# GpSimd's scaling of the attention weights with a second operation, K's late half not at step 4 for the fifth pair, and the last pair of a group coupling one step later

## The chip, the cores and the metric

The kernel runs on one core of one Trainium2 chip. The metric is the device time of one execution in microseconds (us), and the time before is the median of three runs. The core's engines work side by side, each through its own list of instructions in order: TensorE (PE in the profile, its weight loads PEld), VectorE (DVE), ScalarE (ACT), GpSimd (POOL) and SyncE (SP), which starts DMAs. ScalarE starts some DMAs too.

## The reference

One layer of a hybrid decoder, 512 tokens by 1024 channels, all in float32. Cut to what matters here:

```python
h = rms_norm(x, norm_mix_pre)
z_rwkv, z_nsa, z_gate = split(h @ w_in)
# RWKV-7, 16 heads of 64
z = z + (prev - z) * mu                        # prev: the token before
r, k, v, ... = split(z)
state = state * w_t + (state @ a_t) b_t + v_t k_t ;  y_t = state @ r_t
# sparse attention, 16 heads of 64: compressed, selected, window
p_c = masked_softmax(s_c);  p_s = masked_softmax(s_s);  p_w = masked_softmax(s_w)
o_b = gb[0] * (p_c @ v_cmp) + gb[1] * (p_s @ vg) + gb[2] * (p_w @ vwb)
m = sigmoid(g_a) * (o_a @ w_branch_rwkv) + sigmoid(g_b) * (o_b @ w_branch_nsa)
x = x + rms_norm(m @ w_out, norm_mix_post)
u_gate, u_val = split(causal_dwconv(rms_norm(x) @ ffn_up))
x = x + rms_norm((silu(u_gate) * u_val) @ ffn_down)
```

With 512 tokens there are 8 blocks of 64 and all of them are selected, and the window of 512 reaches every earlier token, so the selected and the window branch are both full causal attention, each with keys and values of its own.

## The kernel before, in words

**Precision.** A float32 product is made of three matmuls on split operands: high weight by high input, high weight by low input, low weight by high input (lines 306, 307, 308, for each of 8 slices k of the contraction). The weights come by DMA as float32 in halves of 512 columns and are split by `split_to`: ScalarE copies the high part (L124), GpSimd subtracts to get the low part (L162). Three buffers of each kind go round.

**Stages.** After the norm come the small projections, then, in one long stage, the projections of RWKV's r, k and v for eight pairs of heads (a pair is 128 columns), with the RWKV scan in chunks of 64 tokens in two groups of four pairs (GP = 4) running beside them and beside the projections of the gates (`gsteps`, tiles gt0.. and gt1..), of attention's keys (`khl`, tiles kst) and of its queries. Then come attention, eight pairs of heads one after the other (`score`, `values`), the merge with w_out, and the gated FFN.

**What orders the work.** The Python code is made of generators. One list of them, the fill, holds projections, whose step is one k, so three matmuls. Other generators (`prep`, `couple`, `invert`, `recur`, `finish`) run as threads beside the fill: for each step of the fill a thread advances by its rate (0.6 for couple). A `yield` more in a thread thus puts what follows some projection matmuls later. From the resulting sequence a scheduler makes each engine's list; an instruction given to `keep_in_program_order` stays where the code has put it, others may be moved a little. PSUM is handed out in tiles of one bank: the projections (k, r, v, gt, kst) share a small pool, and a new tile takes the bank that was released first.

**What the change touches.**
- `inputs(p)` (from L493) projects k, r and v of pair p. Token shift is done at the eviction in two halves: `shift_a` on ScalarE writes K = (1 - mu) k (L333), `shift_b` on VectorE adds mu times the token before, from the same PSUM bank (L336). For K, `shift_b` is issued at step SK = 4 of r's projection and kept there. R and V have both halves right at their eviction.
- `couple` (L581) makes of a pair's tiles what the scan needs: it multiplies AR's second half on GpSimd, yields twice, then transposes V (tiles pv, L140), multiplies KB by AR on TensorE (tiles g, L605), masks the products on VectorE (L608) and sends two kinds of blocks by DMA (ld and l2, L617 and L618). AR's first half was made on VectorE in `prep` (L570). After it come more transposes (pt), the tile LV and the tile bv with its DMA bvd.
- `invert` inverts the triangular blocks of a group: four loads of XL (L650), which read the ld blocks back, a copy into PSUM on ScalarE (XP, L655), and a chain of multiplications and additions on VectorE (L660, L662) that is covered by projections.
- `gsteps` projects a gate and evicts it on ScalarE (L478) with a store behind it on ScalarE's queue (gtd, L479).
- `score` (L1051) handles two heads of attention. Per query block of 128 it makes the scores, subtracts the maximum and takes the exponential of both branches (tiles p, 512, 384, 256 or 128 columns); `norm` (L1063) then scales each p in place by one number per row, its gate divided by its sum, which lies in a small tile stt: the selected branch on VectorE, the window branch on GpSimd, both at L1073. `values` transposes p (tiles pt, L140) and multiplies by the values (o, L1146). The compressed branch (sc, L1037 to L1049) runs beside it on VectorE and GpSimd, and its transposes are the tile pct.

Of the kernel before, what the change touches and what calls it, by code (L numbers as in the profile page):

```python
# [13 lines left out]
OP = mybir.AluOpType  # L14
# [18 lines left out]
GP = 4  # L33
PR, CR, IY, FR = 0.6, 0.5, 31, 0.5
ID, IE, RD, RR, NG0, NQ1, PX, FN = (30, 30), (54, 54), (67, 67), (1.05, 0.85), 8, 4, 3, 1.15
NW, NU, PA, SK = 13, 3, 0.25, 4
# [6 lines left out]
def hybrid_layer(ctx: ExitStack, tc: tile.TileContext, a, out, dbg=None, stop=None):  # L43
# [288 lines left out]
    def shift_a(p, o, mc, n=128):  # L332
        sc.activation(o, p[:n], AF.Copy, scale=omm[:n, mc:mc + 1])  # L333
# [159 lines left out]
    def inputs(p, o):  # L493
        K = o.K = rw.tile([128, S], F32, tag="K", name=f"K{p}", bufs=2)
        pk = pj(f"k{p}")
        yield from proj_steps(4 + 3 * p, f"k{p}", pk)
        shift_a(pk, K, 8 + p)
        R = o.R = rw.tile([128, S], F32, tag="R", name=f"R{p}", bufs=1)
        pr = pj(f"r{p}")
        for i, _ in enumerate(proj_steps(3 + 3 * p, f"r{p}", pr)):  # L500
            if i == SK:
                tc.keep_in_program_order(shift_b(pk, K, 8 + p))
            yield
        shift(pr, R, p)
        VW = o.VW = rw.tile([128, 64 + S], F32, tag="V", name=f"V{p}", bufs=1)
        po.memset(VW[:, 0:64], 0.0)
        pv = pj(f"v{p}")
        yield from proj_steps(5 + 3 * p, f"v{p}", pv)
        shift(pv, VW[:, 64:], 16 + p)
        o.lh = rw.tile([128, 256], F32R, tag="lh", name=f"lh{p}", bufs=1)  # L510
        o.ll = rw.tile([128, 256], F32R, tag="ll", name=f"ll{p}", bufs=1)
        split_to(a["lwa"][p], o.lh, o.ll, f"lw{p}", 256)
# [68 lines left out]
    def couple(p, o, gr, i):  # L581
        R, VW, Q, EC, KB = o.R, o.VW, o.Q, o.EC, o.KB
        AR = gr.AR[i]

        if Q is not None:
            sc.activation(AR[:, 0, :], Q, AF.Copy)
        po.tensor_tensor(AR[:, 1, :].rearrange(c8, t=64), R.rearrange(c8, t=64), EC[:, :, 1:65], op=OP.mult)
        sc.activation(gr.Dc[:, i], EC[:, :, 64], AF.Copy)
        yield
        yield  # L590
        for q in range(2):
            pv = px(f"pv{p}{q}")
            for j in range(4):
                c = 4 * q + j
                tr(pv[:, j * 128:(j + 1) * 128], VW[:, c * 64:c * 64 + 128], ident)
            pvv = pv.rearrange("p (c h f) -> p c h f", h=2, f=64)
            sc.activation(gr.UV[64:128, 4 * q:4 * q + 4, i], pvv[64:128], AF.Copy)
        m4 = mask.rearrange("p (s t) -> p s t", t=64)[:, None].to_broadcast([128, 4, 2, 64])
        for q in range(2):
            gh = [(pz, py)[q](f"g{p}{q}{h}") for h in range(2)]  # L600
            for j in range(4):
                c = 4 * q + j
                for h in range(2):
                    hs = slice(h * 64, (h + 1) * 64)
                    te.matmul(gh[h][:, j * 128:(j + 1) * 128], KB[hs, c].rearrange("p s t -> p (s t)"),  # L605
                              AR[hs, :, c * 64:(c + 1) * 64], start=True, stop=True)
            for h in range(2):
                ve.tensor_tensor(gr.GS[:, 0:2 + i:1 + i, 4 * q:4 * q + 4, h].rearrange("p s c t -> p c s t"),  # L608
                                 gh[h].rearrange("p (c s t) -> p c s t", s=2, t=64), m4, op=OP.mult)
            po.tensor_tensor(KB[:, 4 * q:4 * q + 4].rearrange("p c s t -> p c (s t)"),  # L610
                             KB[:, 4 * q:4 * q + 4].rearrange("p c s t -> p c (s t)"),
                             EC[:, 4 * q:4 * q + 4, 64:65].to_broadcast([128, 4, 128]), op=OP.mult)
        yield
        yield
        for b in range(2):
            bs = slice(b * 32, (b + 1) * 32)
            sy.dma_start(gr.ld[b, i].rearrange("c h i t -> i (c h) t"), gr.GS[bs, 0, :, :, bs])  # L617
        sy.dma_start(gr.l2[i].rearrange("c h i t -> i (c h) t"), gr.GS[0:32, 0, :, :, 32:64])  # L618
        yield
        yield  # L620
        pt = [px(f"pt{p}{q}") for q in range(2)]
        for q in range(2):
            for j in range(4):
                c = 4 * q + j
                m = tr(pt[q][:, j * 128:(j + 1) * 128], KB[:, c].rearrange("p s t -> p (s t)"), ident)
                if c == 0:
                    tc.keep_in_program_order(m)
            sc.activation(gr.BKT[i][:, 4 * q:4 * q + 4, :], pt[q].rearrange("p (c f) -> p c f", f=128), AF.Copy)
        pl = py(f"pl{p}")
        for c in range(8):  # L630
            for h in range(2):
                te.matmul(pl[h * 64:(h + 1) * 64, c * 64:(c + 1) * 64], gr.GS[64:128, 0, c, h, :],
                          gr.UV[64:128, c, i, h, :], start=True, stop=True)
        sc.activation(gr.LV[:, i], pl.rearrange(c8, t=64), AF.Copy)
        pbo = py(f"pbo{p}")
        te.matmul(pbo, onesr, o.rbh, start=True, stop=False)
        te.matmul(pbo, onesr, o.rbl, start=False, stop=True)
        bv = rw.tile([128, S], F32, tag="T", name=f"bv{p}", bufs=NT)
        ve.tensor_tensor(bv, pbo, VW[:, 64:], op=OP.mult)
        sy.dma_start(bvd[p], bv)  # L640
        yield
        yield
# [268 lines left out]
    for g in range(2):  # L911
        group_tiles(g)
        for i in range(GP):
            p = GP * g + i
# [136 lines left out]
    def score(p8, o):  # L1051
        kt = kst[p8 // 2]
        cmp_ = compressed(p8, o)
        next(cmp_)
        rh, st = [], []
        for e in range(2):
            h = 2 * p8 + e
            rh.append(nw.tile([128, S], F32, tag="rh", name=f"rh{h}", bufs=4))
            po.tensor_scalar(rh[e], dist, float(2.0 ** (-8.0 * (h + 1) / 16)), 1.0, op0=OP.mult, op1=OP.mult)
            st.append(nw.tile([128, 4, 8], F32, tag="stt", name=f"stt{h}", bufs=4))  # L1060
        o.pe = {}

        def norm(e, qb, k):  # L1063
            sv = st[e].rearrange("p x (b q) -> p x b q", q=4)
            two = slice(qb, qb + 2)
            if k == qb + 1:
                ve.reciprocal(sv[:, 2, :, two], sv[:, 1, :, two])
                ve.tensor_tensor(sv[:, 3, :, two], sv[:, 2, :, two],  # L1068
                                 gates[:, two, 6 * p8 + 3 * e + 1:6 * p8 + 3 * e + 3].rearrange("p q b -> p b q"),
                                 op=OP.mult)  # L1070
            for b in range(2):
                i = b * 4 + k
                (po if b else ve).tensor_scalar(o.pe[e, b, k], o.pe[e, b, k], st[e][:, 3, i:i + 1], None, op0=OP.mult)  # L1073

        done = []
        for e, qb in ((0, 3), (0, 2), (1, 3), (1, 2), (0, 1), (0, 0), (1, 1), (1, 0)):
            h = 2 * p8 + e
            n = (qb + 1) * 128
            qt = qs[p8][e][:, qb * 128:(qb + 1) * 128]
            if qb < 2:  # L1080
                s_ = px(f"s{h}{qb}")
                for x in range(2):
                    te.matmul(s_[:, :2 * n], qt, kt[:, x, :, :n], start=x == 0, stop=x == 1)  # L1083
                parts = [s_[:, b * n:(b + 1) * n] for b in range(2)]
            else:
                parts = []
                for b in range(2):
                    s_ = px(f"s{h}{qb}{b}")
                    for x in range(2):
                        m = te.matmul(s_[:, :n], qt, kt[:, x, b, :n], start=x == 0, stop=x == 1)  # L1090
                        if p8 + x + b == 0:
                            tc.keep_in_program_order(m)
                    parts.append(s_[:, :n])
            for b in range(2):
                sb = nw.tile([128, n], F32, tag=f"p{qb}{b}", name=f"p{h}{qb}{b}", bufs=4 if qb else 3)
                i = b * 4 + qb
                ve.tensor_tensor_reduce(sb, parts[b], rh[e][:, (3 - qb) * 128:], -1.0, BIG, OP.add, OP.min,  # L1097
                                        st[e][:, 0, i:i + 1])
                sc.activation(sb, sb, AF.Exp, scale=-1.0, bias=st[e][:, 0, i:i + 1], accum_out=st[e][:, 1, i:i + 1])  # L1099
                o.pe[e, b, qb] = sb  # L1100
            next(cmp_, None)
            if done:
                norm(*done.pop(0))
            if qb % 2 == 0:
                done += [(e, qb, qb + 1), (e, qb, qb)]
            yield
        for x in done:
            norm(*x)
# [480 lines left out]
```

## Time and profile before

| | |
|---|---|
| median of three runs | 1169.26 us (1168.82 to 1169.72) |
| profiled execution | 1168.92 us |
| its span (first to last instruction) | 1167.1 us |
| granted TensorE clock | 0.997 |
| TensorE busy | 1145.0 us, 98% of the span |
| VectorE, ScalarE, GpSimd busy | 587.8, 584.0, 580.5 us, 50% each |
| GpSimd's scaling (L1073) | 64 instructions, 72.9 us |
| VectorE's scaling (L1073) | 64 instructions, 33.2 us |

In a row of groups of instructions stand the line, the engine, the operation, out<-in, (partitions x elements, type) and the count; then the busy time and the mean ns of one, then the idle time of the engine just before them and what ended most of it. In a row of the timeline stand the start in us, the duration, the engine, the line and the operation; in brackets the wait just before it and what ended the wait; rows of several equal instructions carry their count. In a row of the list of waits stand who waited, for whom, the total, the number and the longest. In a row of the table of windows stand the stretch, its length, and the busy time of PE, PEld, DVE, ACT and POOL with their counts, then the granted clock, the DMA engines' busy share and GB/s.

### The profile page before, as it was taken

The numbers are of one execution on the slowest core, as the hardware profiler recorded it, in microseconds if no ns is written. First come the engines' busy times: TensorE is split into PE (matmuls) and PEld (weight loads), VectorE is DVE, ScalarE is ACT, GpSimd is POOL, SyncE is SP. The second block draws the span as 40 slices with busy tenths as digits, with TensorE's granted clock in tenths as the row PEclk, the third lists the DMA queues.
The fourth block names the chain that finished last, engine by engine and source line by source line (L and its number), as shares of the span: only waits on it lengthen the run. The fifth ranks groups of instructions, "written<-read, shape, count | busy, mean of one in ns | idle before, by whom it ended". The sixth has DMA issues, their size and how long they took to land.

```text
span 1167.1 us, 19728 instructions
## 1 busy us (share of the span) xinstructions
PE 1145.0 (98%) x7338; PEld 916.2 (79%) x7338; DVE 587.8 (50%) x1194; ACT 584.0 (50%) x1150; POOL 580.5 (50%) x526
## 2 busy tenths in 40 slices
PE   9999999999999999989999999999999999999997
PEld 7888878777887887656677778889888888888886
DVE  4226666534676642677798745754443343331103
ACT  5537664453666434567676654434444444443311
POOL 4335654425655443477766635511565566554440
PEclk9999999999999999999999999999999999999999
DMA  6433235321433664115552136641233333334421
GB/s 235 126 83 80 84 105 166 111 86 44 133 113 103 190 182 128 56 42 149 168 156 89 46 98 182 211 153 37 83 99 99 95 95 100 99 94 134 135 64 72
DMA packets 95507, 131.95 MB, mean 113 GB/s; under 512 B 34033, under 2 KB 36913, under 8 KB 95154
## 3 DMA queue, kind: packets, MB, share of 16 engines
q1 hardware_dynamic: 79490, 116.26, 33.3%
q10 hardware_dynamic: 15920, 14.42, 4.0%
q8 instruction: 58, 0.95, 0.3%
q14 instruction: 39, 0.32, 0.1%
HBM read 108.30 MB, written 19.14 MB: 109 GB/s over the span
## 4 chain that ended last, share of the span: by engine, by line
PE 91%; DVE 4%; ACT 2%; POOL 2%; issue 1%; DVEq 0%; POOLq 0%; ACTq 0%
PE pu L221 6%; PE pu L223 6%; PE pu L222 6%; PE dn L1321 3%; PE dn L1320 3%; PE dn L1319 3%; PE o L1146 3%; PE pt L140 3%; PE ub L1203 3%; PE gt L306 2%; PE ub L1205 2%; PE ub L1204 2%; PE gt L307 2%; PE gt L308 2%; PE v L306 2%; PE v L307 2%
## 5 line engine op out<-in xcount | busy, mean ns | idle before, releaser
L1099 ACT ACTIVATE p<-p,stt 128x384 f32<-128x384 f32 (+3 forms) x128 | 70.7, 554 | 35.1 <-DVE stt L1097 33.4
L1073 POOL TENSOR_SCALAR p<-p,stt 128x512 f32<-128x512 f32 (+1 forms) x64 | 72.9, 1149 | 30.7 <-DVE stt L1068 16.4
L1461 DVE SCALAR_TENSOR_TENSOR u<-pu,cvec,u 128x511 f32<-128x511 f32 x44 | 33.0, 749 | 101.1 <-ACT u L1460 101.1
L1097 DVE CUSTOM_DVE_ANT_0 p<-s,rh 128x384 f32<-128x384 f32 (+3 forms) x128 | 59.2, 485 | 24.6 <-PE s L1083 18.9
L140 PE MATMUL pt<-ident,p 128*128 128x128 f32 x320 | 44.7, 274 | 2.9 <-POOL p L1073 2.0
L1467 DVE TENSOR_TENSOR al<-u,ah 128x512 fp32r<-128x512 f32 x22 | 23.9, 1085 | 45.5 <-ACT ah L1466 45.5
L140 PEld LDWEIGHTS pt<-ident,p 128*128 128x128 f32 x320 | 37.9, 141 | 7.8 <-POOL p L1073 2.5
L1146 PE MATMUL o<-PT,vt 128*64 128x384 f32 (+3 forms) x256 | 43.9, 448 | 0.0
L1465 POOL TENSOR_TENSOR u<-u,u 128x512 f32<-128x512 f32 x22 | 28.4, 1290 | 27.2 <-DVE u L1462 26.3
L1090 PE MATMUL s<-kst,qs 128*128 128x512 f32 (+1 forms) x128 | 38.5, 390 | 2.6 <-DVE stt L1097 2.4
L1460 ACT ACTIVATE u<-pu,cvec 128x512 f32<-128x512 f32 x44 | 33.6, 765 | 3.0 <-PE pu L1423 3.0
L1462 DVE SCALAR_TENSOR_TENSOR u<-pu,cvec,u 128x510 f32<-128x510 f32 x44 | 33.0, 749 | 1.6
L1073 DVE TENSOR_SCALAR p<-p,stt 128x512 f32<-128x512 f32 (+1 forms) x64 | 33.2, 548 | 0.8
L1137 ACT ACTIVATE PT<-pt 128x512 f32<-128x512 f32 x48 | 27.6, 586 | 9.2 <-PE pt L140 8.8
L1146 PEld LDWEIGHTS o<-PT,vt 128*64 128x64 f32 x256 | 16.8, 136 | 19.4 <-issue 17.5
L1090 PEld LDWEIGHTS s<-kst,qs 128*128 128x128 f32 x128 | 21.4, 189 | 10.7 <-DVE stt L1097 6.2
L1367 DVE TENSOR_TENSOR p2ss<-p2ss 128x1 f32<-128x1 f32 x4 | 0.6, 161 | 52.1 <-ACT p2jl L1365 52.1
L1139 DVE COPY PT<-pt 128x512 f32<-128x512 f32 x32 | 21.6, 676 | 8.3 <-PE pt L140 8.3
L1466 ACT ACTIVATE ah<-u 128x512 fp32r<-128x512 f32 x22 | 13.9, 633 | 22.1 <-POOL u L1465 22.1
L1099 ACT ACTIVATION_READ_ACCUMULATOR p<-p,stt 128x1 f32 x128 | 24.1, 189 | 0.0
L809 ACT ACTIVATE UV<-xs 64x256 f32<-64x256 f32 x16 | 6.0, 378 | 35.0 <-PE xs L804 34.6
L662 DVE TENSOR_TENSOR XP<-XP,TM 128x30 f32<-128x30 f32 (+14 forms) x60 | 20.3, 338 | 2.0
(1758 smaller groups left out, 3939.4 us busy)
## 6 DMA issues: line engine op xcount, KB each, us to landing
gtd<-gt ACTq DMA_DIRECT2D x16, 256.0 KB, 2.8
qs<-qd SPq DMA_DIRECT2D x32, 128.0 KB, 3.3
g<-gtd SPq DMA_DIRECT2D x16, 256.0 KB, 3.0
xt<-in_x_dram SPq DMA_DIRECT2D x4, 512.0 KB, 5.2
bvd<-bv SPq DMA_DIRECT2D x8, 256.0 KB, 2.3
bvl<-bvd SPq DMA_DIRECT2D x8, 256.0 KB, 2.9
kst<-kst ACTq DMA_DIRECT2D x16, 128.0 KB, 2.3
t<-oad SPq DMA_DIRECT2D x8, 256.0 KB, 3.3
```

The source lines that it names most:

```text
L140: return te.transpose(o, i, ident)
L221: te.matmul(p, wh(k), mh(k), start=first and k == 0, stop=False)
L222: te.matmul(p, wh(k), ml(k), start=False, stop=False)
L223: te.matmul(p, wl(k), mh(k), start=False, stop=last and k == n - 1)
L306: te.matmul(p, wh(k), hh[:, k, :], start=k == 0, stop=False)
L307: te.matmul(p, wh(k), hl[:, k, :], start=False, stop=False)
L1073: (po if b else ve).tensor_scalar(o.pe[e, b, k], o.pe[e, b, k], st[e][:, 3, i:i + 1], None, op0=OP.mult)
L1090: m = te.matmul(s_[:, :n], qt, kt[:, x, b, :n], start=x == 0, stop=x == 1)
L1097: ve.tensor_tensor_reduce(sb, parts[b], rh[e][:, (3 - qb) * 128:], -1.0, BIG, OP.add, OP.min, st[e][:, 0, i:i + 1])
L1099: sc.activation(sb, sb, AF.Exp, scale=-1.0, bias=st[e][:, 0, i:i + 1], accum_out=st[e][:, 1, i:i + 1])
L1146: te.matmul(acc[e * 64:e * 64 + 64, j * 128:], vt[:, j, b * 256 + g * 64:b * 256 + g * 64 + 64], m[e][:, c:c + n], start=False, stop=k == ...
L1203: te.matmul(p, wh(k), sh[:, k, :], start=k == 0, stop=False)
```

## The change

Three edits. GpSimd's scaling in `norm` gets a second operation, a multiplication by the constant 1.0; VectorE's stays as it was. In `inputs`, for the first pair of group 1 (p = GP, the fifth pair), K's late half is issued right behind its early half and is not kept at a place. In `couple`, the last pair of each group yields three times instead of twice ahead of pv and g.

```diff
         shift_a(pk, K, 8 + p)
+        if p == GP:
+            shift_b(pk, K, 8 + p)
         R = o.R = rw.tile([128, S], F32, tag="R", name=f"R{p}", bufs=1)
         pr = pj(f"r{p}")
         for i, _ in enumerate(proj_steps(3 + 3 * p, f"r{p}", pr)):
-            if i == SK:
+            if i == SK and p != GP:
                 tc.keep_in_program_order(shift_b(pk, K, 8 + p))
             yield
...
         sc.activation(gr.Dc[:, i], EC[:, :, 64], AF.Copy)
-        yield
-        yield
+        for _ in range(3 if i == GP - 1 else 2):
+            yield
         for q in range(2):
             pv = px(f"pv{p}{q}")
...
             for b in range(2):
                 i = b * 4 + k
-                (po if b else ve).tensor_scalar(o.pe[e, b, k], o.pe[e, b, k], st[e][:, 3, i:i + 1], None, op0=OP.mult)
+                w = st[e][:, 3, i:i + 1]
+                if b:
+                    po.tensor_scalar(o.pe[e, b, k], o.pe[e, b, k], w, 1.0, op0=OP.mult, op1=OP.mult)
+                else:
+                    ve.tensor_scalar(o.pe[e, b, k], o.pe[e, b, k], w, None, op0=OP.mult)
```

The rows below are the engines' lists, in which a tile's name ends in a running number; lines of the changed kernel are two higher from `couple` on. First TensorE where pair 3, the last of group 0, couples beside the gate gt10 (pv3 the transposes of V, g3 the products), before:

```order
L306 MATMUL gt10_1690<-hh_72,gt10h1_1697 128x512
L307 MATMUL gt10_1690<-hl_73,gt10h1_1697 128x512
L308 MATMUL gt10_1690<-hh_72,gt10l1_1698 128x512
L140 MATMUL pv30_1720<-ident_89,V3_1527 128x128 x4
L140 MATMUL pv31_1726<-ident_89,V3_1527 128x128 x4
L605 MATMUL g300_1732<-AR03_860,KB3_1665 128x128
L605 MATMUL g301_1733<-AR03_860,KB3_1665 128x128
```

and now:

```order
L306 MATMUL gt10_1690<-hh_72,gt10h1_1697 128x512
L307 MATMUL gt10_1690<-hl_73,gt10h1_1697 128x512
L308 MATMUL gt10_1690<-hh_72,gt10l1_1698 128x512
L306 MATMUL gt10_1690<-hh_72,gt10h1_1697 128x512
L307 MATMUL gt10_1690<-hl_73,gt10h1_1697 128x512
L308 MATMUL gt10_1690<-hh_72,gt10l1_1698 128x512
L140 MATMUL pv30_1726<-ident_89,V3_1527 128x128 x4
L140 MATMUL pv31_1732<-ident_89,V3_1527 128x128 x4
L607 MATMUL g300_1738<-AR03_860,KB3_1665 128x128
L607 MATMUL g301_1739<-AR03_860,KB3_1665 128x128
```

The transposes and the products stand behind six more matmuls of the gate; pair 7 stands likewise to the gate gt06 in group 1.

ScalarE a little later in group 0, around the copy of XP (gt02h and gt12h are high parts of weights, gt01 and gt11 gates, gtd their store), before:

```order
L124 ACTIVATE gt02h0_1963<-gt020r_1965 128x512
L478 ACTIVATE gt01_1846<-gt01_1773 128x512
L479 DMA gtd_110<-gt01_1846 128x512
L655 ACTIVATE XP0_1878<-XL0_1849 128x32x32
L478 ACTIVATE gt11_1959<-gt11_1855 128x512
L124 ACTIVATE gt02h1_1969<-gt021r_1971 128x512
L479 DMA gtd_110<-gt11_1959 128x512
L124 ACTIVATE gt12h0_2003<-gt120r_2005 128x512
```

and now:

```order
L124 ACTIVATE gt02h0_1963<-gt020r_1965 128x512
L478 ACTIVATE gt01_1846<-gt01_1770 128x512
L479 DMA gtd_110<-gt01_1846 128x512
L478 ACTIVATE gt11_1959<-gt11_1855 128x512
L479 DMA gtd_110<-gt11_1959 128x512
L657 ACTIVATE XP0_1878<-XL0_1849 128x32x32
L124 ACTIVATE gt02h1_1969<-gt021r_1971 128x512
L124 ACTIVATE gt12h0_2003<-gt120r_2005 128x512
```

The copy of XP went behind gt11's eviction and its store; group 1 changes in the same way around gt16, gt07 and XP1, ahead of the split for gt17's second half. On TensorE the first matmul of gt12 now stands ahead of gt02's second half's first L308.

VectorE during the inverse of group 0, where R4, K4 and V4 are the late halves of pair 4, before:

```order
L660 TENSOR_TENSOR TM0_1850<-XL0_1849,XP0_1878 128x108
L662 TENSOR_TENSOR XP0_1878<-XP0_1878,TM0_1850 128x4x27
L336 SCALAR_TENSOR_TENSOR R4_2084<-r4_2085,vec_86,R4_2084 128x511
L660 TENSOR_TENSOR TM0_1850<-XL0_1849,XP0_1878 128x84
L662 TENSOR_TENSOR XP0_1878<-XP0_1878,TM0_1850 128x3x28
L660 TENSOR_TENSOR TM0_1850<-XL0_1849,XP0_1878 128x58
L662 TENSOR_TENSOR XP0_1878<-XP0_1878,TM0_1850 128x2x29
L660 TENSOR_TENSOR TM0_1850<-XL0_1849,XP0_1878 128x30
L662 TENSOR_TENSOR XP0_1878<-XP0_1878,TM0_1850 128x30
L336 SCALAR_TENSOR_TENSOR K4_2042<-k4_2043,vec_86,K4_2042 128x511
L336 SCALAR_TENSOR_TENSOR V4_2125<-v4_2127,vec_86,V4_2125 128x511
```

and now:

```order
L664 TENSOR_TENSOR XP0_1878<-XP0_1878,TM0_1850 128x13x18
L662 TENSOR_TENSOR TM0_1850<-XL0_1849,XP0_1878 128x228
L336 SCALAR_TENSOR_TENSOR K4_2042<-k4_2043,vec_86,K4_2042 128x511
L664 TENSOR_TENSOR XP0_1878<-XP0_1878,TM0_1850 128x12x19
L662 TENSOR_TENSOR TM0_1850<-XL0_1849,XP0_1878 128x220
...
L662 TENSOR_TENSOR TM0_1850<-XL0_1849,XP0_1878 128x168
L664 TENSOR_TENSOR XP0_1878<-XP0_1878,TM0_1850 128x7x24
L336 SCALAR_TENSOR_TENSOR R4_2085<-r4_2086,vec_86,R4_2085 128x511
L662 TENSOR_TENSOR TM0_1850<-XL0_1849,XP0_1878 128x150
L664 TENSOR_TENSOR XP0_1878<-XP0_1878,TM0_1850 128x6x25
```

K's late half went from behind the inverse to a place far inside it, and R's a few steps forward. The bank of v4 is that of r4 before and that of k4 now. On SyncE the store bvd stood behind two of the four XL loads and stands behind one now; on ScalarE the square of K that makes Q (L531) goes ahead of the split for v4's second half. In attention no engine's list changes its order.

## The prediction

> **What bounds the kernel now.** I read the page's busy times, then TensorE's own waits, then the stretches in which these waits lie.
>
> ```profile
> PE 1145.0 (98%) x7338; PEld 916.2 (79%) x7338; DVE 587.8 (50%) x1194; ACT 584.0 (50%) x1150; POOL 580.5 (50%) x526
> PE pt L140 <- POOL p L1073: 2.0, 2, 1.3
> PE g L605 <- DVE AR L570: 1.9, 2, 0.9
> 480.00:500.00 20.00, 16.78 (x154) 12.01 (x150) 16.81 (x60) 13.22 (x39) 13.68 (x15) 1.00 0.25 80
> 500.00:520.00 20.00, 17.80 (x94) 12.71 (x94) 13.61 (x44) 14.06 (x36) 13.72 (x16) 1.00 0.17 47
> 640.00:660.00 20.00, 19.84 (x121) 14.22 (x120) 14.95 (x54) 11.94 (x36) 12.49 (x11) 1.00 0.17 52
> ```
>
> TensorE is busy for 98% of the span, the others for half. No edit removes matmuls, so all that can be won is TensorE's waiting. Four of its waits are touched: pt on GpSimd's p, twice, 2.0 us in all, and g on AR, twice, 1.9, shown here (total, times, longest); v on R's eviction, 1.98, and pct on GpSimd's sc, 2.19, shown below. They make 8.1 us. GpSimd's scaling (L1073) stands behind pt and pct, K's late half behind v, the later couple behind g. The windows show that attention's first 40 us hold 5.4 us without a matmul (3.22 + 2.20), a later 20 us only 0.16. A faster GpSimd is thus worth something at the beginning of attention and hardly anything afterwards.
>
> **K's late half for pair 4.**
>
> ```profile
> 197.39 0.39 DVE L660 TENSOR_TENSOR TM<-XL,XP 128x228 f32<-128x228 f32 x1
> 202.24 0.31 DVE L660 TENSOR_TENSOR TM<-XL,XP 128x150 f32<-128x150 f32 x1
> 202.52 0.67 ACT L333 ACTIVATE K<-k,vd 128x512 f32<-128x512 f32 x1
> 207.17 0.39 PE L308 MATMUL r<-hh,r4l 128*128 128x512 f32 x1
> 208.74 0.75 DVE L336 SCALAR_TENSOR_TENSOR R<-r,vec,R 128x511 f32<-128x511 f32 x1 [4.56 <-ACT R L333]
> 209.55 0.50 PE L306 MATMUL v<-hh,v4h 128*128 128x512 f32 x1 [1.98 <-DVE R L336]
> 210.80 0.74 DVE L336 SCALAR_TENSOR_TENSOR K<-k,vec,K 128x511 f32<-128x511 f32 x1
> 216.43 0.75 DVE L336 SCALAR_TENSOR_TENSOR V<-v,vec,V 128x511 f32<-128x511 f32 x1 [4.89 <-ACT V L333]
> ```
>
> The v matmuls wait for R's eviction, while K's late half still reads k's PSUM bank at 210.80, when v has begun: so v sits in r's bank, just vacated, and not in k's, which was complete 5 us earlier. Matmuls of this shape follow each other every 0.23 us, so v could start at 207.40 instead of 209.55. In the new order K's half stands behind the 228-wide multiplication of the inverse. VectorE is there (197.8, or 3 us later by what follows below) before ScalarE ends K's first half at 203.19 (202.52 + 0.67); K is done by 204, 3 us before v wants a bank, and k's is free. **Gain 2.15 us.**
>
> What it costs: VectorE's inverse now stands behind K. From the end of the 228 row to the 150 row it runs 4.5 us, so R's half is reached at about 208.4 and runs at 208.74 as now, when ScalarE has finished R; the rest (202.24 to 210.80 without R's 4.56 and 0.75) takes 3.3 us and ends at 212.8. V's half, next in line, cannot start before 216.43 - 2.15 = 214.3, and it waits 4.89 us now: the inverse stays covered. ScalarE's Q (L531) goes ahead of one weight split, at about 204, where that split starts at 204.7 now: nothing.
>
> **The last pair of each group couples one step later.**
>
> ```profile
> 165.96 1.03 PE L140 MATMUL pv<-ident,V 128*128 128x128 f32 x8
> 167.12 0.68 DVE L570 SCALAR_TENSOR_TENSOR AR<-Q,pb 128x512 f32<-128x512 f32 x1
> 167.95 2.06 PE L605 MATMUL g<-AR,KB 64*128 64x128 f32 x32 [0.95 <-DVE AR L570]
> 182.46 1.03 ACT L655 ACTIVATE XP<-XL 128x1024 f32<-128x1024 f32 x1 [1.11 <-DMA XL<-ld]
> 185.84 0.60 ACT L478 ACTIVATE gt<-gt 128x512 f32<-128x512 f32 x1 [2.36 <-PE gt L308]
> 186.34 0.62 ACT L124 ACTIVATE gt02h<-gt021r 128x512 fp32r<-128x512 f32 x1
> 186.47 0.33 ACTq L479 DMA_DIRECT2D gtd<-gt  x1
> 187.03 1.29 POOL L162 TENSOR_TENSOR gt02l<-gt021r,gt02h 128x512 fp32r<-128x512 f32 x1 [4.80 <-ACT gt02h L124]
> 188.81 0.39 PE L308 MATMUL gt<-hh,gt02l 128*128 128x512 f32 x1
> 389.87 1.29 POOL L162 TENSOR_TENSOR gt17l<-gt171r,gt17h 128x512 fp32r<-128x512 f32 x1 [4.80 <-ACT gt17h L124]
> 391.65 0.39 PE L308 MATMUL gt<-hh,gt17l 128*128 128x512 f32 x1
> ```
>
> Six projection matmuls (6 x 0.23 = 1.37 us) now stand ahead of the transposes and g. AR is ready at 167.80, g would come at about 168.3: the wait of 0.95 us and 0.16 us of a draining pipeline (0.39 - 0.23) go, 1.1 us, and by the second wait in the list as much in group 1.
>
> But the new ScalarE order takes most of it back. XP's copy, which now runs while ScalarE waits for gt11's last matmul, goes behind that gate's eviction and its store. Counted from the eviction at 185.84: the store's issue ends at 186.80, XP takes 1.03 us, the split of gt02's second half starts 1.4 us later than now. Its low half ends at 188.32 now (187.03 + 1.29), 0.5 us ahead of its matmul at 188.81. So TensorE meets a new wait of 0.9 us, less 0.2 for one gt12 matmul that the new order puts ahead of it. In group 1 the same stands at gt17 (391.65 - 391.16 = 0.5 again) with no matmul moved ahead. Net: 1.1 - 0.7 and 1.1 - 0.9, **0.6 us together**. The inverse starts some 3 us later; in group 0 the K wait above and V cover that, in group 1 the wait for the first kst eviction:
>
> ```profile
> 400.19 0.68 DVE L972 TENSOR_TENSOR kst<-ksp,kst 64x512 fp32r<-64x512 f32 x1 [4.00 <-ACT kst L971]
> ```
>
> SyncE's bvd store goes ahead of two more XL loads; XL then comes later by one issue, about 0.45 us, but XP waits for the eviction anyway. GpSimd's rows keep their order there.
>
> **GpSimd's scaling, 64 instructions.**
>
> ```profile
> L1073 POOL TENSOR_SCALAR p<-p,stt 128x512 f32<-128x512 f32 x16 | 27.1, 1691 | 18.7 <-DVE stt L1068 12.1 <-ACT p L1099 6.5
> L1073 POOL TENSOR_SCALAR p<-p,stt 128x384 f32<-128x384 f32 x16 | 20.8, 1300 | 0.0
> L1073 POOL TENSOR_SCALAR p<-p,stt 128x128 f32<-128x128 f32 x16 | 9.7, 605 | 0.0
> L1059 POOL TENSOR_SCALAR rh<-dist 128x512 f32<-128x512 f32 x16 | 10.1, 630 | 5.3 <-DVE stt L1097 4.0 <-PE y L760 0.5
> 493.41 2.90 POOL L1073 TENSOR_SCALAR p<-p,stt 128x512 f32<-128x512 f32 x2 [2.31 <-ACT p L1099]
> 496.37 0.44 PE L140 MATMUL pt<-ident,p 128*128 128x128 f32 x2 [0.67 <-POOL p L1073]
> 496.51 1.43 DVE L1073 TENSOR_SCALAR p<-p,stt 128x512 f32<-128x512 f32 x2
> 496.88 2.95 POOL L1073 TENSOR_SCALAR p<-p,stt 128x512 f32<-128x512 f32 x2
> 499.89 0.33 PE L140 MATMUL pt<-ident,p 128*128 128x128 f32 x1 [1.34 <-POOL p L1073]
> 515.96 3.00 POOL L1073 TENSOR_SCALAR p<-p,stt 128x512 f32<-128x512 f32 x2 [5.01 <-DVE stt L1068]
> 519.70 0.42 DVE L1044 TENSOR_REDUCE sct<-sc 128x8 f32<-128x256 f32 x1 [2.02 <-POOL sc L1041]
> 520.92 0.62 POOL L1049 TENSOR_TENSOR sc<-sc,sct 128x256 f32<-128x256 f32 x1 [1.25 <-DVE stt L1067]
> 521.60 0.63 PE L140 MATMUL pct<-ident,sc 128*64 128x128 f32 x4 [2.19 <-POOL sc L1049]
> ```
>
> No row has a scalar from memory and two operations. The nearest are L1073 itself (scalar from memory, one operation: 1691 ns, and (1691 - 605) / 384 = 2.83 ns per element) and L1059 (two operations with constants, the same 512: 630 ns). I take 630: the second operation is what the edit adds, and L1059 is the same multiplication twice; a slope of 2.83 for one input looks like a loop that is not the fast one. Ends of the range: no change (1691), and above, a second pass that costs as much per element again.
>
> [...]
>
> A pair of 512 and 384 falls from 2.99 to about 1.16 us (384 by L1059's slope: 0.53). At 493 to 500 the two waits for p (0.67 and 1.34) go, until VectorE's share of the same head bounds: it ends at 497.94, two transposes take 0.22, so 499.89 becomes 498.2 at best. I take 1.5, as ScalarE's evictions move less. At 516 the chain is pair, sc, VectorE's reduction, sc, transposes: it shortens by 1.83 and VectorE's 2.02 with it; I take 1.6 of the 2.19. **Gain 3.1 us**; between 0 and 4.2 (2.0 + 2.2) at this price.
>
> **Sum.** 2.15 + 0.6 + 3.1 = 5.85 us. The profiled execution took 1168.92 us (span 1167.1 and 1.8 around it), so 1163.1; the median of the runs lies 0.34 above it: **1163.4 us**.
>
> **Rivals.**
> (B) GpSimd gets fast, but ScalarE or VectorE holds TensorE a moment later. For: VectorE is busy 16.81 of 20 us there. Against: it falls to 13.61 in the next 20. Half of the 3.1 lost: 1165.0.
> (C) The price of L1073 does not change, since the scalar from memory is what makes it slow. 1169.26 - 2.75 = 1166.5. For: L1059 differs in both respects. [...]
> (D) Slower: the second operation doubles the slope. A pair grows by 896 x 2.83 = 2.5 us, and three pairs lie on the path (493, 497, 516): +7.6. Later GpSimd, busy 12.49 of 20, gets 6 more and is nearly full; about 1 us in each of six steps: 1169.26 - 2.75 + 7.6 + 6 = 1180. It decides from a pair that is 0.9 us longer, where 3 x 0.9 eats the 2.75. Against: L1059.
> (E) The reordered work gives all of its 2.75 back, VectorE standing still for K while others queue: 1166.2 with a fast GpSimd.
>
> **Chances and range.** Forecast 0.53, B 0.17, C 0.14, E 0.09, D 0.07. About 0.2% (2.3 us, below 1166.9) is what a measurement can tell from no change; C and E lie just past it, so half of each counts as the same. Faster 0.53 + 0.17 + 0.12 = 0.82, same 0.11, slower 0.07. If every wait in question went, 8.1 us plus 1.4 of draining (some eight gaps of 0.16 and a little), the time would be 1159.8; upwards the range takes in C and E: 1159.5 to 1167.0.
>
> **What the new profile would show.** L1073 on GpSimd near 630 ns for 512; TensorE's list of waits without v L306 and g L605, without pt on p, and pct under 0.6; new waits of 0.7 to 0.9 us at gt02l and gt17l. I am wrong if L1073 stays at 1691, or if s or o in attention wait more than now.

## The result, and the profile after

The changed kernel takes **1161.69 us** (median of four runs, 1160.68 to 1162.85) against 1169.04 (median of four, 1168.27 to 1169.72) on the same chips: a ratio of 0.9938, 95% interval 0.9920 to 0.9955. Timed once more, its median was 1162.44 and the ratio 0.9947 (0.9934 to 0.9960). Forecast were 1163.4, between 1159.5 and 1167.0. The runs of one kernel mostly fall into two groups some 2 us apart, which in the profiled executions go with how soon TensorE's matmuls get faster in the first 15 us (its first split projection starts at 12.4 to 12.8 us or at 14.2 to 14.8, last section), so that a median shifts with the mix; places are compared below by the traces.

The profiled execution took 1162.85 us, 6.07 less than that of before, span 1161.1. First the page's busy times:

```profile
PE 1144.0 (99%) x7338; PEld 915.2 (79%) x7338; DVE 587.8 (51%) x1194; ACT 582.6 (50%) x1150; POOL 544.1 (47%) x526
```

Then TensorE's list of waits (total, times, longest):

```profile
PE pct L140 <- POOL sc L1051: 0.8, 1, 0.8
...
PE gt L308 <- POOL gt17l L162: 0.6, 1, 0.6
...
PE pct L140 <- DVE stt L1070: 0.6, 1, 0.6
...
PE gt L308 <- POOL gt02l L162: 0.3, 1, 0.3
```

TensorE's work is the same; the waits for p on GpSimd, for AR and for R's late half are gone, that for sc fell from 2.2 to 0.8. New are gt17l, gt02l, a second wait of pct and one of 0.7 of pg for VectorE, while the scores' waits (s) fell from 2.4 to 2.2. Next pair 4's late halves on VectorE with the inverse's last addition, and v's first matmul:

```profile
203.12 0.75 DVE L336 SCALAR_TENSOR_TENSOR K<-k,vec,K 128x511 f32<-128x511 f32 x1 [1.98 <-ACT K L333]
...
207.30 0.39 PE L306 MATMUL v<-hh,v4h 128*128 128x512 f32 x1
...
208.63 0.75 DVE L336 SCALAR_TENSOR_TENSOR R<-r,vec,R 128x511 f32<-128x511 f32 x1 [0.47 <-ACT R L333]
...
212.56 0.20 DVE L664 TENSOR_TENSOR XP<-XP,TM 128x30 f32<-128x30 f32 x1
...
214.01 0.75 DVE L336 SCALAR_TENSOR_TENSOR V<-v,vec,V 128x511 f32<-128x511 f32 x1 [1.25 <-ACT V L333]
```

K's half is done at 203.87, v starts at 207.30 without a wait, R's half comes later than v's start and holds nothing up; the inverse ends at 212.76, before V's half is due. Then the coupling in group 0, on TensorE, ScalarE and GpSimd, with gt17 of group 1 below:

```profile
168.18 2.06 PE L607 MATMUL g<-AR,KB 64*128 64x128 f32 x32
...
184.69 0.60 ACT L478 ACTIVATE gt<-gt 128x512 f32<-128x512 f32 x1 [4.50 <-PE gt L308]
...
185.82 1.03 ACT L657 ACTIVATE XP<-XL 128x1024 f32<-128x1024 f32 x1 [0.54 <-ACT gt L478]
...
186.98 0.39 PE L308 MATMUL gt<-hh,gt02l 128*128 128x512 f32 x1
...
187.47 1.28 POOL L162 TENSOR_TENSOR gt02l<-gt021r,gt02h 128x512 fp32r<-128x512 f32 x1 [6.39 <-ACT gt02h L124]
...
188.81 0.50 PE L308 MATMUL gt<-hh,gt02l 128*128 128x512 f32 x1 [0.34 <-POOL gt02l L162]
...
387.63 0.39 PE L308 MATMUL gt<-hh,gt17l 128*128 128x512 f32 x1
...
389.48 0.50 PE L308 MATMUL gt<-hh,gt17l 128*128 128x512 f32 x1 [0.63 <-POOL gt17l L162]
```

g now follows the transposes with no wait. But two matmuls that stand 0.68 us apart undisturbed stand 1.83 apart at gt02 (0.23 of it is the gt12 matmul put between) and 1.85 at gt17. Last the scaling on GpSimd, for the widest and the narrowest tile:

```profile
L1077 POOL TENSOR_SCALAR p<-p,stt 128x512 f32<-128x512 f32 x16 | 12.9, 808 | 22.8 <-DVE stt L1070 20.3 <-ACT p L1105 2.3
...
L1077 POOL TENSOR_SCALAR p<-p,stt 128x128 f32<-128x128 f32 x16 | 6.0, 375 | 0.0
```

and three landmarks of attention on TensorE, the second pair's pc, its pct, and the first matmul of q5 on low weights, with one scaling on GpSimd that is needed below:

```profile
496.63 1.05 PE L1029 MATMUL pc<-kcs,qs 128*128 128x64 f32 x8
...
516.65 0.86 POOL L1077 TENSOR_SCALAR p<-p,stt 128x512 f32<-128x512 f32 x1
516.72 0.63 PE L140 MATMUL pct<-ident,sc 128*64 128x128 f32 x4 [0.76 <-POOL sc L1051]
...
526.15 0.50 PE L308 MATMUL q<-hh,q5l 128*128 128x512 f32 x1 [0.88 <-POOL q5l L162]
```

Of before the same three are these:

```profile
500.08 1.06 PE L1027 MATMUL pc<-kcs,qs 128*128 128x64 f32 x8
...
521.60 0.63 PE L140 MATMUL pct<-ident,sc 128*64 128x128 f32 x4 [2.19 <-POOL sc L1049]
...
532.40 0.51 PE L308 MATMUL q<-hh,q5l 128*128 128x512 f32 x1 [0.88 <-POOL q5l L162]
```

**Where the time went.** The same matmuls stand in every kernel, so the time gained between two of them can be read off. The table takes seven of them from the timelines (of before: the first of gt10 at 162.56, the last of gt12 at 196.29, the first of v4 at 209.55, the last of gt17 at 393.69, and the three above) and gives, in us, by how much a kernel is faster than before in each stretch between. A minus is a loss.

| kernel | to gt12 | to v4 | to gt17 | to pc | to pct | to q5 |
|---|---|---|---|---|---|---|
| changed | -0.01 | 2.15 | -0.21 | 1.41 | 1.43 | 1.37 |
| changed, again | -0.06 | 2.15 | -0.18 | 1.42 | 1.45 | 1.38 |
| only GpSimd | -0.02 | 0.01 | -0.03 | 1.42 | 1.44 | 1.39 |
| only K | 0.02 | 2.16 | 0.17 | -0.14 | -0.13 | 0.52 |
| only the coupling | -0.02 | 0.01 | -0.47 | 0.01 | -1.56 | 0.51 |
| without the coupling | 0.00 | 2.16 | 0.05 | 1.41 | 1.48 | 1.38 |
| XP kept ahead | 1.04 | 2.15 | 0.30 | 1.43 | 1.48 | 1.37 |
| XP ahead, loads later | 1.04 | 2.15 | 1.19 | 1.44 | 1.49 | 1.38 |
| first two pairs only | -0.03 | 2.16 | -0.16 | 1.42 | 1.49 | 1.38 |
| scaling left out | -0.04 | 2.15 | -0.19 | 1.72 | 2.15 | 1.28 |
| K not kept in place | 0.00 | 2.15 | 0.10 | -0.12 | 0.00 | 0.51 |
| K at step 0, kept | -0.03 | 0.01 | -0.03 | 0.02 | -1.53 | 0.52 |

For the changed kernel the six make 6.14; with 0.11 won ahead of gt10 and 0.18 lost after q5 that is the 6.07 between the executions.

### The profile page after: what moved, and what is told of

It reads as the page before. It is cut to its first block, busy times and chain, and to the rows that moved or that the text cites. A ratio compares the mean times of both kernels' runs of the same rounds, so it can differ in the third digit from the quotient of the medians.

```text
span 1161.1 us, 19727 instructions
## 1 busy us (share of the span) xinstructions
PE 1144.0 (99%) x7338; PEld 915.2 (79%) x7338; DVE 587.8 (51%) x1194; ACT 582.6 (50%) x1150; POOL 544.1 (47%) x526
## 4 chain that ended last, share of the span: by engine, by line
PE 52%; DVE 1%; POOL 1%; issue 0%; ACT 0%; DVEq 0%; POOLq 0%; ACTq 0%
PE pu L221 6%; PE pu L222 6%; PE pu L223 6%; PE dn L1327 3%; PE dn L1325 3%; PE dn L1326 3%; PE o L1152 3%; PE ub L1209 3%; PE ub L1211 2%; PE ub L1210 2%; PE pt L140 2%; PE s L1096 1%; PE wo L1399 1%; PE wo L1398 1%; PE wo L1397 1%; PE s L1089 1%
## 5 line engine op out<-in xcount | busy, mean ns | idle before, releaser
L1077 POOL TENSOR_SCALAR p<-p,stt 128x512 f32<-128x512 f32 (+1 forms) x64 | 38.7, 615 | 38.8 <-DVE stt L1070 22.3
```

What stands on the lines that cost most here:

```text
L1077: po.tensor_scalar(o.pe[e, b, k], o.pe[e, b, k], w, 1.0, op0=OP.mult, op1=OP.mult)
```

## Experiments

**Each edit alone.** Starting from the changed kernel, two of the three edits are undone (for GpSimd's the call reads as before; the others as on the minus lines of the change).

> Only GpSimd's second operation, the other two edits undone. Theory (the three gains stand in three places and add up): 512 columns take 808 ns as in the changed kernel, the waits for p on GpSimd go, pct's falls from 2.2 to under 0.9, and the time is 1169.0 - 2.8 = 1166.2 (1.4 us at 497 to 500 and 1.4 us at 517 to 522, the two steps by which attention comes earlier in the changed kernel). Rival (the edits work together): attention starts at the old place in a different state, and the gain is under 1.5 us, above 1167.5. Second rival: the measured 7.3 us lie mostly in attention, and this alone gives 4 us or more, below 1165.

> Only K's late half for pair 4. Theory: v4 takes k4's bank, its wait for R's late half (1.98 us) goes with the draining, 1169.0 - 2.15 = 1166.9, and the first v4 matmul starts at 207.4. Rival: with XP's copy at its old place the inverse starts earlier, VectorE reaches K's half earlier or later than in the changed kernel, and part of the wait stays: 1168.

> Only the later coupling of the last pair. Theory from the two traces: the wait of g goes in both groups (1.0 us each), and the waits for the weight splits of gt02 and gt17 (0.3 and 0.6 with their draining, 0.9 and 1.2 us) take it back: 1169.0 within 0.5. As predicted before the result it would be 0.6 faster, 1168.4. Rival: it also moves later work to better places and is worth over 1.5 us: below 1167.5.

Measured, against 1169.11 for before on the same chip: GpSimd alone 1163.72, ratio 0.9953 (0.9940 to 0.9967); K alone 1166.01, 0.9978 (0.9967 to 0.9989); the coupling alone 1169.88, 1.001 (1.000 to 1.002). K gives its 2.15 by the trace, wherever it is made. The coupling gives nothing in group 0 and loses half a microsecond in group 1; its median lies somewhat above the 1169.0 within 0.5 that was expected. GpSimd's 5.4 in the medians is more than the theory's 2.8. By the table there is a third step, to q5, and before has lost some more there to a lowered clock (last section): 4.2 in all, so the second rival, 4 us or more, is nearest. The profiled executions are 3.85 apart (1168.92 and 1165.07); where the rest of the medians' difference lies is not shown.

The third step is a wait that the profile of before doesn't have. In the run with the coupling alone TensorE's waits from pct to q5 are these, with two rows of GpSimd and VectorE between:

```profile
523.57 1.73 POOL L1075 TENSOR_SCALAR p<-p,stt 128x512 f32<-128x512 f32 x1
523.64 0.63 PE L140 MATMUL pct<-ident,sc 128*64 128x128 f32 x4 [2.19 <-POOL sc L1049]
...
526.57 0.75 DVE L885 SCALAR_TENSOR_TENSOR y<-y,vec,pg 128x512 f32<-128x512 f32 x1 [2.10 <-POOL y L876]
...
527.37 0.73 PE L1087 MATMUL s<-kst,qs 128*128 128x512 f32 x2 [0.99 <-DVE y L885]
...
533.93 0.50 PE L308 MATMUL q<-hh,q5l 128*128 128x512 f32 x1 [0.88 <-POOL q5l L162]
```

The scores wait 1.0 us for a product of VectorE; the same wait is in the runs with K alone, K not kept in place and K at step 0, and in none with the fast form. The product in turn waits for a sum on GpSimd (L876), and this stands behind one scaling of 512 columns: 1.73 us at 523.57, where the changed kernel's takes 0.86 at 516.65. So the third step is a GpSimd scaling on the path as well. Without the wait the stretch is shorter by 10.29 - 9.43 = 0.86 us, as much as that scaling is. In before's profile the clock was lowered there instead (0.72, 0.50 and 0.93 granted in the windows of 2 us from 522 to 528), which cost 1.37 (10.80 - 9.43) in place of 0.86.

**The changed kernel without the coupling.**

```diff
-        for _ in range(3 if i == GP - 1 else 2):
-            yield
+        yield
+        yield
```

> The changed kernel without the later coupling. Theory: the coupling is worth nothing, so this stands within 0.5 of the changed kernel (1161.7): 1161.2 to 1162.2, with the wait of g back (twice 0.95) and the waits for gt02 and gt17 gone. Rival: the coupling carries a part of the 7.3 us that the two other edits do not explain, and this is at 1163 or above.

1162.43, ratio 0.9940 (0.9928 to 0.9953), beside 0.9938 and 0.9947 for the changed kernel; it was expected at 1161.2 to 1162.2. g waits again (1.9 in all), gt02l and gt17l don't. The coupling is worth nothing as it stands; by the table it costs 0.3.

**The changed kernel again.**

> The changed kernel once more, for its time with more runs and a second profile. The four runs shown lie at 1160.7 to 1160.8 and at 1162.6 to 1162.9. Theory: its median is 1161.7 within 0.6. If the stretch of lowered clock in the profile of before (0.91 in 520 to 540) is what made the difference there larger, then a second profile of the changed kernel shows such a stretch somewhere, or the ratio moves to about 0.995.

1162.44, a little above the bound. Its second profile shows no stretch of lowered clock at the start of attention either (no projection matmul takes more than 0.50 us there, last section); the ratio moved to 0.9947, which fits the second half of what was expected, not the first, though its interval overlaps the earlier one.

**XP's copy kept ahead of the eviction.** One dependency without a wait (added by `nosync`) makes the scheduler put gt11's and gt07's eviction behind XP's copy on ScalarE:

```diff
-        sc.activation(XP.rearrange("u i c -> u c i"), LU, AF.Copy)
+        gr.xp = sc.activation(XP.rearrange("u i c -> u c i"), LU, AF.Copy)
...
-        evict(sc.activation(g, p, AF.Tanh, scale=0.5))
+        m = evict(sc.activation(g, p, AF.Tanh, scale=0.5)); i in (3, 14) and nosync(m, G[i > 3].xp)
```

> The changed kernel with XP's copy kept ahead of the gate's eviction on ScalarE in both groups, as before the change. Theory (the copy's new place is what takes the later coupling's gain back): no wait of gt on gt02l and gt17l, 0.9 and 1.2 us earlier, so 2.0 us faster than the changed kernel. Rival: the split comes late for another reason (the raw weights' DMA behind the XL loads, or the eviction itself), the waits stay, and the time is the same.

1160.70, ratio 0.9936 (0.9923 to 0.9949), 1.74 below the changed kernel. Group 0 gains the full 1.05. Group 1 gains 0.5 of the 1.3 that were lost there, and a wait is left. ScalarE, SyncE and TensorE there:

```profile
379.22 0.42 SPq L934 DMA_DIRECT2D dist<-in_dist_dram  x1
...
380.69 0.43 SPq L158 DMA_DIRECT2D gt171r<-in_wf_dram  x1
...
382.11 1.03 ACT L657 ACTIVATE XP<-XL 128x1024 f32<-128x1024 f32 x1 [2.39 <-DMA XL<-ld]
...
384.21 0.60 ACT L478 ACTIVATE gt<-gt 128x512 f32<-128x512 f32 x1 [1.07 <-PE gt L308]
...
385.81 0.63 ACT L124 ACTIVATE gt17h<-gt171r 128x512 fp32r<-128x512 f32 x1 [1.01 <-DMA gt171r<-in_wf_dram]
...
387.87 0.50 PE L308 MATMUL gt<-hh,gt17l 128*128 128x512 f32 x1 [0.52 <-POOL gt17l L162]
```

ScalarE is in time now, but the raw weights aren't: the later coupling has also put three loads for attention (dist, cdist, cmask) ahead of gt17's second half on SyncE's queue, where they stood behind it before, so the weights' issue comes 1.5 us later.

**The three loads behind the weights again.** Their DMAs move into a step of the fill after the gates:

```diff
-    sy.dma_start(dist, a["dist"])
-    sy.dma_start(cdist, a["cdist"])
-    sy.dma_start(cmask, a["cmask"])
+    def loads():
+        for t, n in ((dist, "dist"), (cdist, "cdist"), (cmask, "cmask")):
+            sy.dma_start(t, a[n])
+        yield
...
-    drive(itertools.chain(*gates_(16 - 6 - NG0, zp), *fr1, ...
+    drive(itertools.chain(*gates_(16 - 6 - NG0, zp), loads(), *fr1, ...
```

> The changed kernel with XP's copy ahead of the gate's eviction (as in the run before) and the three loads of dist, cdist and cmask issued behind the second half of gt17's raw weights on SyncE, as in the kernel before. Theory: in group 1 the wait for gt17's split that is left (0.52 us, the raw weights' DMA being late by three issues) goes, with its draining 0.7 us: 0.7 faster than the run with XP alone (1160.7), 1160.0, and 2.3 faster than the changed kernel by the trace at gt17's last matmul. Rival: the raw weights wait for the three XL loads as well, the wait stays, 1160.7.

**1159.50**, ratio 0.9923 (0.9909 to 0.9937): the lowest median here, 1.2 below the last, which was timed on another chip, and the two intervals overlap. By the trace the stretch to gt17 gains 0.89 more, the split comes right behind the eviction, and gt17's matmuls run without a wait:

```profile
383.08 0.62 ACT L124 ACTIVATE gt17h<-gt171r 128x512 fp32r<-128x512 f32 x1
...
385.56 0.39 PE L308 MATMUL gt<-hh,gt17l 128*128 128x512 f32 x1
```

The later coupling is thus worth 1.0 in group 0 and, beside the kernel without it (0.05), 1.1 in group 1, once what it displaces is put back.

**Forms of GpSimd's scaling.** Each pair of heads has a form of its own, on lines of their own (1078 for pair 0, 1080 for pair 1, and so on by twos).

> The changed kernel with another form of GpSimd's scaling in each of the eight pairs of heads, for the price of each; the pairs with a constant or with the factor twice compute another scaling. Pair 0: number per row alone; 1: number per row, then times 1.0; 2: times 1.0, then number per row; 3: number per row, then plus 0.0; 4: constant alone; 5: constant, then times 1.0; 6: a product of two tensors, the number per row spread over the columns; 7: number per row twice. Theory A (one operation is the slow form, whatever the number's source): pairs 0 and 4 near 1690 ns for 512, pairs 1, 2, 3, 5, 7 near 630 to 810. Theory B (a number from memory is slow unless a constant stands beside it): pair 0 and pair 7 near 1690, pair 4 near 630. Pair 6 near 1190, as the other products on GpSimd.

```profile
L1078 POOL TENSOR_SCALAR p<-p,stt 128x512 f32<-128x512 f32 x2 | 3.3, 1650 | 2.3 <-ACT p L1120 2.3
...
L1080 POOL TENSOR_SCALAR p<-p,stt 128x512 f32<-128x512 f32 x2 | 1.8, 888 | 5.2 <-DVE stt L1070 5.2
...
L1082 POOL TENSOR_SCALAR p<-p,stt 128x512 f32<-128x512 f32 x2 | 1.6, 780 | 0.6 <-DVE stt L1070 0.6
...
L1084 POOL TENSOR_SCALAR p<-p,stt 128x512 f32<-128x512 f32 x2 | 1.8, 894 | 2.1 <-DVE stt L1070 2.1
...
L1086 POOL TENSOR_SCALAR p<-p 128x512 f32<-128x512 f32 x2 | 3.1, 1530 | 1.9 <-ACT p L1120 1.9
...
L1088 POOL TENSOR_SCALAR p<-p 128x512 f32<-128x512 f32 x2 | 1.4, 716 | 1.4 <-ACT p L1120 1.4
...
L1090 POOL TENSOR_TENSOR p<-p,stt 128x512 f32<-128x512 f32 x2 | 2.3, 1158 | 2.6 <-DVE stt L1070 2.6
...
L1092 POOL TENSOR_SCALAR p<-p,stt 128x512 f32<-128x512 f32 x2 | 1.9, 967 | 2.7 <-ACT p L1120 2.0 <-DVE stt L1070 0.7
```

One execution, 1167.00 us. Theory A holds: one operation is the slow form, with a constant (1530) as with a number from memory (1650). With two operations it takes 716 to 967, whatever the second one is and wherever the numbers come from; three of the five lie above the 810 that was expected. The order of the two and the source make 100 to 250 ns, about as much as one form differs by itself (0.69 to 0.94 us for 512 columns in the changed kernel), and two instructions carry each row, so their shares are not shown.

**The fast form in the first two pairs only.**

```diff
-                if b:
+                if b and p8 < 2:
                     po.tensor_scalar(o.pe[e, b, k], o.pe[e, b, k], w, 1.0, op0=OP.mult, op1=OP.mult)
+                elif b:
+                    po.tensor_scalar(o.pe[e, b, k], o.pe[e, b, k], w, None, op0=OP.mult)
```

> The changed kernel with the two-operation form only in pairs 0 and 1 of attention, the other six as before (16 of the 64 instructions changed). Theory: the whole gain lies in the first two pairs, so 1162.4 as the changed kernel, within 0.4, with no wait of pt or pct on GpSimd later. Rival: the later pairs carry a part (GpSimd is 36 us less busy, of which these two pairs make 9): 1163.5 or above.

1160.76, ratio 0.9940 (0.9927 to 0.9954): not slower than the changed kernel, and in the table the six stretches make 6.26 beside its 6.14. Sixteen instructions bring the whole gain. The other 48 keep the old price,

```profile
L1079 POOL TENSOR_SCALAR p<-p,stt 128x512 f32<-128x512 f32 x12 | 20.2, 1684 | 11.4 <-DVE stt L1070 11.3
```

and no wait of TensorE on them appears.

**No scaling on GpSimd** (the window branch's weights stay unscaled).

> The changed kernel without GpSimd's scaling (the window branch's weights stay unscaled): what a scaling of no cost at all would give. Theory: with 808 ns GpSimd is off the path nearly everywhere, and only pct's waits (0.8 + 0.6) are left to win: 0.5 to 1.4 us faster than the changed kernel. Rival: GpSimd still sets the pace in attention: 3 us or more.

1162.18, ratio 0.9942 (0.9928 to 0.9956). In the table the steps to pc and pct rise from 1.41 to 1.72 and from 1.43 to 2.15, and 0.6 is lost after q5: a scaling for nothing would bring 0.9 up to q5 and some 0.6 at the end.

**K's late half: the place or the keeping.** From the kernel before, once issued at step 4 but not kept in place, once at step 0 and kept.

```diff
             if i == SK:
-                tc.keep_in_program_order(shift_b(pk, K, 8 + p))
+                m = shift_b(pk, K, 8 + p)
+                if p != GP:
+                    tc.keep_in_program_order(m)
```

> The kernel before, with K's late half for pair 4 issued at step 4 as before but not kept in place. The scheduler then puts it inside the inverse on VectorE. Theory: leaving out the keeping is what works, not the place in the code: v4's wait for R's late half goes, and v4 starts 2.15 us earlier (207.4 after the same start). Rival: the place in the code counts, K comes too late for v4's bank, and v4 starts at 209.5.

```diff
-            if i == SK:
+            if i == (0 if p == GP else SK):
```

> The kernel before, with K's late half for pair 4 issued at step 0 and kept in place. On VectorE it still stands behind the whole inverse. Theory: nothing changes, the wait of v4 for R's late half stays at 2.0 us, 209.5. Rival: an earlier place helps by itself: v4 earlier by 1 us or more.

One profile each: 1164.72 and 1168.05. Not kept, K's half runs at 201.59 and v4 starts with no wait, 2.15 earlier after the same work; kept at step 0, it runs after R's and nothing is won:

```profile
201.59 0.75 DVE L336 SCALAR_TENSOR_TENSOR K<-k,vec,K 128x511 f32<-128x511 f32 x1 [3.60 <-ACT K L333]
...
205.77 0.39 PE L306 MATMUL v<-hh,v4h 128*128 128x512 f32 x1
```
```profile
207.73 0.50 PE L306 MATMUL v<-hh,v4h 128*128 128x512 f32 x1 [1.99 <-DVE R L336]
...
208.98 0.74 DVE L336 SCALAR_TENSOR_TENSOR K<-k,vec,K 128x511 f32<-128x511 f32 x1
```

Both absolute times are early because these executions' first split projection starts some 2 us sooner (12.81 and 12.60, in before 14.73). What holds K behind the inverse is the keeping, not the step at which it is issued.

## Why the prediction was right, and which terms were not

| term | forecast | measured |
|---|---|---|
| K's late half | 2.15 | 2.15 |
| the later coupling | 0.6 | -0.2 |
| GpSimd's scaling | 3.1 | 4.2, of which 0.5 by before's lowered clock |
| sum | 5.85 | 6.15; profiled execution 6.07 |

That the sum came so close is in part luck: 0.8 too much for the coupling and 1.1 too little for GpSimd nearly cancel.

**K's late half** went step by step as told: K done by 204 (203.87), v at 207.4 (207.30), the inverse at 212.8 (212.76), V's half still waiting.

**The coupling** is the term that failed. The gain at g was right (1.02 in each group; 1.1 forecast), and so was the cause of the loss, XP's copy behind the eviction, which the run with XP kept ahead shows. Its size was not: 1.05 instead of 0.7 in group 0, 1.3 instead of 0.9 in group 1. The matmul of gt12 put ahead did fill 0.23 of the wait in group 0, as reckoned. But the matmul on gt02l came 1.15 us late (1.83 - 0.68), not 0.9, as XP's copy started 1.13 us after the eviction's start (185.82 and 184.69) where 0.96 had been allowed, and the matmul 0.06 after the split's end; group 1 is alike. And behind each of the two waits the matmuls lose another 0.13: those on gt02l start at 188.81, 189.61 and 190.30 and those on gt17l at 389.48, 390.27 and 390.97, where they stand 0.68 apart undisturbed. "SyncE's bvd store ... XP waits for the eviction anyway" looked at XP only: what SyncE's new order delayed in group 1 was gt17's weights, hidden behind XP in the changed kernel and seen once XP was out of the way.

**GpSimd's scaling** was right in mechanism and place, wrong in price: 808 ns for 512, not 630; the forms show why 630 was near and not it (716 for two constants in this place, where L1059's row has 630). The pair at 493 takes 1.50 us, not 1.16. Yet each of the two steps gave the whole shortening of its pair (2.9 to 1.5, 1.4 gained), where I had allowed 1.5 and 1.6 of 1.83. What was missing is the third step of 0.86: one more scaling on the path, ahead of GpSimd's sum for y. Before's profile shows no wait of TensorE for it, because the clock was lowered in the same stretch (0.50 from 524 to 526) and TensorE's own work lasted longer.

Of the rivals, C (the number from memory makes it slow) and D (the second operation doubles the slope) fall with the forms. B would show in a smaller first step, which there isn't; what VectorE and ScalarE hold back is seen only when the scaling costs nothing. E is half true: the coupling's reorder took back all of its own gain, but nothing of K's 2.15. One operation and two cost differently with either source: 1650 ns against 888 with the number per row, 1530 against 716 with constants.

The medians fell by 7.35 where the profiles give 6.07; the second comparison has 6.3.

## What to carry to other kernels

When the bound engine is 98% busy, list its waits and price each edit by the waits that it ends: here 16 of 64 instructions on a half-idle engine were worth 4 us and the other 48 nothing. When work moves by one step, write down for each queue it passes what now stands behind it, and ask of each when it is needed; an edit that nets nothing may be a good edit with two displaced neighbours. On GpSimd, try a float32 scaling with a second operation (808 ns against 1691 for 512 columns here).

## What the runs showed of the hardware

**One operation took longer than two on GpSimd.** The scaling by the number per row: 1691 ns against 808 for 512 columns, and per column (1691 - 605) / 384 = 2.83 ns against (808 - 375) / 384 = 1.13.

**A lowered clock at the start of attention.** All six profiles in which pair 0 scales in the slow form (before, only K, only the coupling, the forms, K not kept, K at step 0) have a stretch of lowered clock between 492 and 528. The windows show it in four of them, with a granted clock of 0.50 in those of 2 us that lie wholly inside. In the forms the matmuls show it (0.63 us for one of a projection, 0.39 outside), and in only K two of the scores at 494.42 (1.08 us, 0.70 in the changed kernel). None of the eight with the fast or no scaling there has one: the windows of three (changed, first two pairs, XP ahead with the loads later) are at 1.00, and in all eight no projection matmul there takes more than 0.50 us. Two windows of before and one of the run with the coupling alone (granted clock third from the end):

```profile
522.00:524.00 2.00, 2.00 (x14) 1.53 (x12) 0.42 (x1) 0.92 (x2) 2.00 (x2) 0.72 0.00 0
524.00:526.00 2.00, 2.00 (x3) 0.50 (x2) 1.48 (x6) 0.76 (x4) 1.92 (x3) 0.50 0.27 24
```
```profile
502.00:504.00 2.00, 2.00 (x7) 1.57 (x6) 2.00 (x9) 1.99 (x3) 1.67 (x2) 0.58 0.00 0
```

In the table it costs between 0.1 us (K not kept, where TensorE's wait for p behind it, 1.34 in before, is gone) and 1.56 (only the coupling). In the four with windows the clock lost there adds up to 1.7 us (in before, from windows of 2 us: 0.56 + 1.00 + 0.14), which is 3.4 us at 0.50; in the forms it lasts some 10 us, from 493.4 to 503.4, and there is one more from 517 to 521, where pair 1 scales in the fast form already. A stretch is found in just the profiles with the slow form in pair 0, but what brings it on is not shown. Of the 3.4 us ahead of it in before, the wait of 2.19 us that ends at 521.60 takes some two thirds. But ahead of three of the six (only K, K not kept, the forms) lie only waits of 0.58 and 0.67 us, while the changed kernel has 0.64 and 0.59 at the same place and no stretch. Nor is it TensorE's busy time alone: that was 1.3 to 2.1 us of the 3.4 ahead of the six, but 1.7 in the 3.4 from 206.03 in the run with K at step 0, with no stretch behind.

**Two starts.** In some executions TensorE's matmuls get faster sooner than in others: its four of line 119 take 3.78 us together (before, changed) or 1.98 (first two pairs, XP ahead with the loads later), and the first split projection starts at 14.2 to 14.8 or at 12.4 to 12.8. First the changed kernel, then the run with the first two pairs:

```profile
5.30 3.78 PE L119 MATMUL gb<-g1r 1*128 1x512 f32 x4
...
14.36 0.68 PE L241 MATMUL b<-hh,b0h 128*128 128x256 f32 x1
```
```profile
5.11 1.98 PE L119 MATMUL gb<-g1r 1*128 1x512 f32 x4
...
12.38 0.68 PE L241 MATMUL b<-hh,b0h 128*128 128x256 f32 x1
```

What decides between the two starts, some 2 us apart, is not shown. By gt10 at most 0.3 of the 2 us has been made up. Of the profiled executions with an early start two have other runs of their kernel beside them: 1160.29 is the least of five for the first two pairs (highest 1162.28), and 1158.70 stands with 1158.52 below 1160.30 and 1160.35 for XP ahead with the loads later.
